# Conformer-conv statistics and output scaling in a hybrid decoder step: ScalarE's copies of blocks 5 and 7 moved, sums 56 columns wide, another order of the final scaling

## The chip, the cores and the metric

The kernel runs on one core of one Trainium2 chip. The metric is the time of one execution in microseconds on the device. The engines are TensorE (PE), VectorE (DVE), ScalarE (ACT), GpSimd (POOL) and SyncE (SP), which only issues DMAs here. Each engine works through its own instructions in order; they wait for one another by semaphores.

## The reference, cut to what matters

Four decoder layers, each a mixer and a squared-ReLU MLP, run over 256 prompt tokens and 8 sample tokens (T = 264 columns) with 1024 channels. The changed code is in the third layer's mixer, the Conformer conv, and in the norm at the very end.

```
def conformer_conv_mixer(xn, state, w_pw1, b_pw1, conv_w, conv_b, ln_g, ln_b, w_pw2, b_pw2):
    ag = jnp.einsum('bld,de->ble', xn, w_pw1) + b_pw1
    a, g = jnp.split(ag, 2, axis=-1)
    buf = jnp.concatenate([state, a * jax.nn.sigmoid(g)], axis=1)
    z = causal_dwconv(buf, conv_w) + conv_b          # 31 taps in each channel
    z = layer_norm(z, ln_g, ln_b)                    # mean and variance over the channels
    y = jnp.einsum('ble,ed->bld', jax.nn.silu(z), w_pw2) + b_pw2
    return y, buf[:, -(CONV_C_W - 1):]
...
return rms_norm(x, norm_final_g), ...
```

## The kernel before

Channels lie on the 128 partitions in eight blocks (0 to 7) and tokens along the columns. Every dense product is made of three TensorE products: weights and activations are each split into a high and a low part (`whi`, `wlo`, `xh`, `xl`). ScalarE makes the high part of a weight piece (L119), and VectorE or GpSimd the low part (L120). The program is written out by hand: in each engine's queue the instructions stand in the order in which the code issues them.

The stage of the change is the second half of `mixer_c`. Blocks 0 to 3 are convolved on VectorE, tap after tap (L855, `do_taps`). Blocks 4 to 7 are convolved on TensorE by 64 products (`conv_step`, L926, numbered n = 0 to 63), sixteen for each block, into two PSUM tiles `pairs[e, 0]` and `pairs[e, 1]`. The loop over n also hands out the other engines' work: it asks for so many taps at each n, for some leftover transposes and their copy to `rows` with two output DMAs on GpSimd's queue (L528, L829, L830), and for two pieces of weights (L119 and L120).

How a block leaves the TensorE convolution: in `leave(e)` ScalarE copies, from each of the two PSUM tiles, the half that lies on the wrong partitions to `over` (L954), and VectorE then adds both halves into `d` (L957). `apart(e)` subtracts a first estimate `mu` of the mean (L970 on VectorE, L972 on GpSimd; L975 for the eight sample columns), ScalarE squares the result (L977), and GpSimd adds up differences and squares over the blocks to `dsum` and `qsum` (L985). Blocks 3 and 7 are not added in; they go to the sums by themselves.

Then comes the norm. `token_sums` (L996) takes the sums over the channels on TensorE: the data are the weights of the product, and a block of ones, 28 or 56 columns wide, is streamed through. Few columns are needed; one of each width is read. VectorE turns the sums into mean and variance of each token (L1066 to L1072 and `rsqrt`, L255 to L259, whose root is ScalarE's). `to_channels` (L1003) spreads the mean (to `wide`) and the root (to `scale`) back over the partitions. `keep_clock` (L1183) issues products of ones with ones, 128 columns each, whose result nobody reads. ScalarE copies `wide` to `mu` (L1074); blocks 0 and 1 are corrected by VectorE from `wide` (L1081), the others by GpSimd from `mu` (L1083). `normed` and `gated` scale (L1088), take the sigmoid (L1090), multiply and split each block, and `wave` (L344 to L347) multiplies six output blocks by `w_pw2` as each input block arrives.

`root_table` is a one-element square root on ScalarE, which brings in the table of that function ahead of time; the sigmoid needs another table.

The end: after the last MLP the squares of the last block (`sq`) and of all others (`acc`) are summed in PSUM tile `ss` (L1284), the root `rt` is made, and six pieces of 128 x 512 are scaled (VectorE L1296 for the left halves from SBUF, ScalarE L1298 for the right halves from PSUM) and written out by SyncE's queue (L1300), the sample rows by ScalarE's (L1302).

Of the kernel before, what the change touches and what calls it, by code (L numbers as in the profile page):

```python
# [26 lines left out]
def decoder_trunk(ctx: ExitStack, tc: tile.TileContext, i, o):  # L27
# [796 lines left out]
    def mixer_c(ready):  # L824
# [122 lines left out]

        def leave(e):


            over = tmp.tile([P, SEQ], F32, tag="t1", name="over")
# [10 lines left out]
        total_ = {}  # L962

        def apart(e):
# [10 lines left out]
            nc.gpsimd.tensor_tensor(out=dt[e][:, SEQ:], in0=zs[:, e, :], in1=mu[:, SEQ:], op=ALU.subtract)  # L975
# [36 lines left out]
        for n, step in enumerate(steps):  # L1012
            conv_step(*step)
            if n == 15:
                leave(4)
                double(NB - 1)
# [6 lines left out]
            if n == 58:  # L1023
                root_table()
            for at, e in ((33, 5), (49, 6)):
# [28 lines left out]
        wide = psum()
        warm = ptp.tile([P, 512], F32, tag="tp", name="warm")
        keep_clock(5, warm)
        token_sums(sums[0], widths[0], 0, "d")
        token_sums(sums[1], widths[1], 0, "q")
        token_sums(sums[0], widths[0], 1, "d3")
        token_sums(sums[1], widths[1], 1, "q3")  # L1060
        token_sums(sums[0], widths[0], 2, "d7")
        token_sums(sums[1], widths[1], 2, "q7")
        dq = [
            ps[:, 0:9 * w].rearrange("p (b r w) -> p b r w", r=3, w=w)[:, :, :, 0] for ps, w in zip(sums, widths)
        ]
# [225 lines left out]
    for b in range(3):
        scale = rt[:, b:b + 1]
        for h, part in enumerate((ys[b][:, 0:512], back[1, b])):
            s = slice(h * 512, (h + 1) * 512)
            if h == 0:
                nc.vector.tensor_scalar_mul(ys[b][:, s], part, scale)  # L1296
            else:
                nc.scalar.activation(ys[b][:, s], part, AF.Copy, scale=scale)  # L1298
            if b < 2:
                nc.sync.dma_start(out=o["y_prompt"][0, b * P:(b + 1) * P, s], in_=ys[b][:, s])  # L1300
        if b == 2:
            nc.scalar.dma_start(out=o["y_sample"].rearrange("b l d -> (b l) d"), in_=ys[b][120:128, :])  # L1302


# [29 lines left out]
```

## Time and profile before

| | |
|---|---|
| median of 3 runs | 1105.05 us (1103.83 to 1105.38) |
| the profiled execution | 1103.74 us, its span 1102.0 us |
| mean granted TensorE clock | 0.992 |
| busy: PE, DVE, ACT, POOL | 99%, 67%, 56%, 18% |
| conv products on PE | 552.27 to 581.5 us |
| first product of `wave` | 598.04 us |
| last dense product | 1091.8 us |
| DMA during the sums | idle from 582 to 587 us |

The span runs from the first to the last instruction; the execution takes 1.7 us more. A stretch that PE spends on small products or waiting is what matters here, since elsewhere PE runs dense products without a gap. The columns of the table of stretches are busy time in us (and number of instructions) of each engine, then the granted clock, where 1.00 is 2.4 GHz and 0.50 is 1.2 GHz. In a timeline a row is a run of equal instructions: its start, the time that the run takes, engine, line, operation, tiles and count, and in brackets how long the engine was idle before it and what ended that.

### The profile page before, as it was taken

How to read it: one execution, taken by the hardware profiler on the slowest of the kernel's cores; microseconds unless marked ns; L12 is line 12 of the kernel's file. 1: busy time of each engine (PE TensorE's matmuls, PEld its weight loads, DVE VectorE, ACT ScalarE, POOL GpSimd, SP SyncE). 2: the span in 40 equal slices, each digit the busy share in tenths (PEclk: the TensorE clock that was granted, in tenths of full speed). 3: DMA queues.
4: the chain of work that ended last, by engine and by line, in shares of the span. 5: the costliest groups of instructions: out<-in, count | busy, mean ns of one | idle time of the engine just before them, and what ended most of it. 6: DMA issues, size and time to landing. Idle time of an engine off the chain costs nothing.

```text
span 1102.0 us, 21950 instructions
## 1 busy us (share of the span) xinstructions
PE 1090.5 (99%) x8801; PEld 1081.7 (98%) x8801; DVE 741.9 (67%) x1461; ACT 612.9 (56%) x1301; POOL 202.7 (18%) x372
## 2 busy tenths in 40 slices
PE   9999999999999999999999999999999999999997
PEld 8999999999999999999988999999999999999996
DVE  5788865566569657766986696566668678646731
ACT  6566653565458536555855585366545467535642
POOL 6213520100220001314993200000101120000010
PEclk9999999999999999999998999999999999999998
DMA  8766756555507666554531186555546565565511
GB/s 256 254 205 204 244 189 188 178 172 179 166 5 254 210 200 198 188 181 147 171 86 36 39 277 220 158 187 191 177 139 218 163 185 192 177 190 170 192 39 40
DMA packets 182639, 189.10 MB, mean 172 GB/s; under 512 B 3505, under 2 KB 180833, under 8 KB 182513
## 3 DMA queue, kind: packets, MB, share of 16 engines
q1 hardware_dynamic: 181865, 185.58, 53.2%
q0 software_dynamic: 656, 2.09, 0.6%
q8 instruction: 69, 1.13, 0.4%
q14 instruction: 33, 0.27, 0.1%
q10 hardware_dynamic: 16, 0.03, 0.0%
HBM read 186.27 MB, written 2.89 MB: 172 GB/s over the span
## 4 chain that ended last, share of the span: by engine, by line
PE 92%; DVE 3%; POOL 2%; ACT 1%; issue 0%; DVEq 0%; ACTq 0%; POOLq 0%
PE mm L160 28%; PE mm L162 28%; PE mm L161 28%; DVE mm L855 2%; POOL wlo L120 1%; PE mm L346 1%; PE mm L344 1%; PE mm L347 1%; PE mm L1183 1%; POOL mat L811 1%; PE warm L1183 0%; ACT mat L818 0%; PE mm L504 0%; PE st L276 0%; PE mm L698 0%
## 5 line engine op out<-in xcount | busy, mean ns | idle before, releaser
L119 ACT CAST whi<-wst 128x512 fp32r<-128x512 f32 x692 | 386.8, 616 | 249.7 <-PE mm L161 234.0
L120 DVE TENSOR_TENSOR wlo<-wst,whi 128x512 fp32r<-128x512 f32 x652 | 430.2, 704 | 103.2 <-ACT whi L119 95.3
L160 PE MATMUL mm<-xh,whi 128*128 128x264 f32 x1512 | 433.2, 286 | 0.0
L162 PE MATMUL mm<-xh,wlo 128*128 128x264 f32 x1512 | 429.2, 284 | 0.0
L161 PE MATMUL mm<-xl,whi 128*128 128x264 f32 x1512 | 428.0, 283 | 0.0
L160 PE MATMUL mm<-uh,whi 128*128 128x264 f32 x1168 | 332.5, 285 | 0.0
L162 PE MATMUL mm<-uh,wlo 128*128 128x264 f32 x1168 | 331.6, 284 | 0.0
L161 PE MATMUL mm<-ul,whi 128*128 128x264 f32 x1168 | 331.2, 284 | 0.0
L161 PEld LDWEIGHTS mm<-xl,whi 128*128 128x128 f32 x1512 | 285.0, 188 | 0.2
L160 PEld LDWEIGHTS mm<-xh,whi 128*128 128x128 f32 x1512 | 284.3, 188 | 0.4
L162 PEld LDWEIGHTS mm<-xh,wlo 128*128 128x128 f32 x1512 | 284.2, 188 | 0.0
L160 PEld LDWEIGHTS mm<-uh,whi 128*128 128x128 f32 x1168 | 220.0, 188 | 0.2 <-DVE xall L538 0.2
L161 PEld LDWEIGHTS mm<-ul,whi 128*128 128x128 f32 x1168 | 219.7, 188 | 0.0
L162 PEld LDWEIGHTS mm<-uh,wlo 128*128 128x128 f32 x1168 | 219.6, 188 | 0.0
L246 POOL TENSOR_TENSOR acc<-acc,sq 128x264 f32<-128x264 f32 x62 | 53.1, 856 | 551.2 <-ACT sq L245 550.4
L1129 DVE SCALAR_TENSOR_TENSOR t<-mm,r 128x264 f32<-128x264 f32 x128 | 54.8, 428 | 63.9 <-PE mm L162 63.7
L228 ACT CAST uh<-u 128x264 fp32r<-128x264 f32 x144 | 59.5, 413 | 33.0 <-DVE u L593 29.0
L1135 ACT ACTIVATE u<-t 128x264 f32<-128x264 f32 x128 | 54.0, 422 | 40.1 <-DVE t L1129 40.0
L230 DVE TENSOR_TENSOR ul<-u,uh 128x264 fp32r<-128x264 f32 x144 | 62.3, 433 | 0.3
L536 DVE TENSOR_TENSOR xall<-mm,xall 128x264 f32<-128x264 f32 x48 | 20.6, 429 | 58.7 <-PE mm L162 58.7
L233 ACT ACTIVATE xh<-xall,pv 128x264 fp32r<-128x264 f32 x56 | 28.9, 515 | 46.0 <-DVE xall L536 29.9
L120 POOL TENSOR_TENSOR wlo<-wst,whi 128x512 fp32r<-128x512 f32 x40 | 51.2, 1305 | 11.8 <-ACT whi L119 11.7
(236 smaller groups left out, 729.2 us busy)
## 6 DMA issues: line engine op xcount, KB each, us to landing
wst<-in_mlp_w_dram SPq DMA_DIRECT2D x128, 1024.0 KB, 5.6
wst<-in_a_w_in_dram SPq DMA_DIRECT2D x23, 1024.0 KB, 5.2
wst<-in_c_w_pw_dram SPq DMA_DIRECT2D x12, 1024.0 KB, 5.3
wst<-in_a_w_out_dram SPq DMA_DIRECT2D x8, 1024.0 KB, 5.2
xin<-in_x_prompt_dram SPq DMA_DIRECT2D x2, 512.0 KB, 6.8
wst<-in_b_w_group_dram SPq DMA_DIRECT2D x1, 1024.0 KB
out_y_prompt_dram<-ys SPq DMA_DIRECT2D x4, 256.0 KB, 2.3
stc<-in_state_conv_c_dram SPq DMA_DIRECT2D x2, 480.0 KB, 7.3
```

The source lines that it names most:

```text
L119: nc.scalar.copy(hi[:, k:k + 2], st[:, k:k + 2])
L120: (nc.gpsimd if u == 3 or (u, k) in ((0, 2), (0, 6)) else lo_engine[0]).tensor_tensor(out=lo[:, k:k + 2], in0=st[:, k:k + 2], in1=hi[:, k: ...
L160: nc.tensor.matmul(ps[:, :n], hi[:, k, s], xh[:, :n], start=first, stop=False)
L161: nc.tensor.matmul(ps[:, :n], hi[:, k, s], xl[:, :n], start=False, stop=False)
L162: nc.tensor.matmul(ps[:, :n], lo[:, k, s], xh[:, :n], start=False, stop=last)
L228: nc.scalar.copy(h, src)
L230: lambda: nc.vector.tensor_tensor(out=l, in0=src, in1=h.bitcast(F32), op=ALU.subtract)
L233: nc.scalar.activation(h, src, AF.Copy, scale=g)
L246: nc.gpsimd.tensor_tensor(out=acc, in0=acc, in1=sq, op=ALU.add)
L855: nc.vector.scalar_tensor_tensor(out=z(e), in0=gb[e][:, t:t + SEQ], scalar=col("ccw", t * 8 + e), in1=z(e), op0=ALU.mult, op1=ALU.add,)
L1129: nc.vector.scalar_tensor_tensor(out=t1, in0=ps[:, :T], scalar=0.0, in1=r, op0=ALU.max, op1=ALU.mult)
L1135: nc.scalar.activation(u, t1, AF.Square)
```

## The change

- In the conv loop ScalarE's copies to `over` are split from `leave` as `come_over(e)` and issued right when the block's last product is issued (n = 15, 31, 47, 63); VectorE's part of `leave` follows at n = 16, 36 and 49 and, for block 7, at the end as before. Before, both stood at n = 15, 33, 49 and at the end, there behind `apart(3)`.
- `apart(0)` and `apart(1)` move from n = 24 and 26 to 32 and 34, `apart(5)` from 38 to 37, `apart(6)` from 55 to 50. The sample columns of blocks 2, 3 and 7 are subtracted at n = 38. The square-root table is asked for at n = 49 instead of 58.
- All `token_sums` are 56 columns wide; there are 2 + 1 + 1 keep-clock products among them instead of 5 ahead, then 3 and 6 instead of 4 and 7. The PSUM tiles of the sums, of `wide` and of the keep-clock products change places.
- The sigmoid's table is asked for right behind the root, ahead of the copy of `wide`.
- At the end the two groups of sums get PSUM tiles of their own, four of the six scalings are VectorE's (one of them from PSUM), ScalarE issues one output DMA itself, and the sample rows go out by SyncE's queue.

```
         def come_over(e):
+            over_[e] = tmp.tile([P, SEQ], F32, tag="t1", name="over")
             for s in range(2):
                 own, other = (slice(h * HALF, (h + 1) * HALF) for h in (s, 1 - s))
-                nc.scalar.copy(over[own], pairs[e, s][other, 1:SEQ + 1])
+                nc.scalar.copy(over_[e][own], pairs[e, s][other, 1:SEQ + 1])
...
+            for at, e in ((15, 4), (31, 5), (47, 6), (63, 7)):
+                if n == at:
+                    come_over(e)
-            for at, e in ((33, 5), (49, 6)):
+            for at, e in ((36, 5), (49, 6)):
                 if n == at:
                     leave(e)
...
-            for at, e in ((22, 4), (24, 0), (26, 1), (38, 5), (55, 6)):
+            for at, e in ((22, 4), (32, 0), (34, 1), (37, 5), (50, 6)):
                 if n == at:
                     apart(e)
...
+        keep_clock(2, warm)
+        for at, e in enumerate(("", "3", "7")):
+            for ps, what in zip(sums, "dq"):
+                token_sums(ps, width, at, what + e)
+            if at < 2:
+                keep_clock(1, warm)
...
         rsqrt(v, root, rz)
+        nc.scalar.activation(scratch, ones[:, 0:1], AF.Sigmoid)
         nc.scalar.copy(mu, wide[:, :T])
-        keep_clock(4, warm)
+        keep_clock(3, warm)
         scale = pst.tile([P, T], F32, tag="st", name="scale")
         to_channels(scale, rz)
-        keep_clock(7, warm)
+        keep_clock(6)
...
-    ss = pst.tile([P, T], F32, tag="st", name="st")
+    ss = [pst.tile([P, T], F32, tag="st", name="st"), ptp.tile([P, 512], F32, tag="tp", name="st2")]
...
+    for b, h in ((0, 0), (0, 1), (1, 0), (1, 1), (2, 0), (2, 1)):
+        scalar = (b, h) in ((0, 1), (2, 1))
...
+            (nc.scalar if scalar else nc.sync).dma_start(
+                out=o["y_prompt"][0, b * P:(b + 1) * P, h * 512:(h + 1) * 512], in_=out
+            )
+    nc.sync.dma_start(out=o["y_sample"].rearrange("b l d -> (b l) d"), in_=ys[2][120:128, :])
```

ScalarE's queue in the conv loop, before, from the square of block 4 on (`gb4<-d4` is the square of block 4; `over` with two different PSUM tiles `mm` are the copies of one block, first block 5, then block 6):

```order
L977 ACTIVATE gb4_6681<-d4_7410 128x264
L977 ACTIVATE gb0_6677<-d0_7406 128x264
L977 ACTIVATE gb1_6678<-d1_7407 128x264
L528 COPY rows_7071<-tp_7519 128x512
L954 COPY over_7569<-mm_7503 64x256
L954 COPY over_7569<-mm_7529 64x256
L119 CAST whi_7392<-wst_7213 128x512
L977 ACTIVATE gb5_6682<-d5_7411 128x264
L119 CAST whi_7392<-wst_7213 128x512
L954 COPY over_7617<-mm_7564 64x256
L954 COPY over_7617<-mm_7593 64x256
```

The same queue at the same place after the change:

```order
L986 ACTIVATE gb4_6681<-d4_7410 128x264
L528 COPY rows_7071<-tp_7519 128x512
L955 COPY over_7551<-mm_7495 64x256
L955 COPY over_7551<-mm_7529 64x256
L986 ACTIVATE gb0_6677<-d0_7406 128x264
L986 ACTIVATE gb1_6678<-d1_7407 128x264
L119 CAST whi_7392<-wst_7213 128x512
L986 ACTIVATE gb5_6682<-d5_7411 128x264
L119 CAST whi_7392<-wst_7213 128x512
L955 COPY over_7614<-mm_7555 64x256
L955 COPY over_7614<-mm_7596 64x256
```

The copies of block 5 and the row copy have passed the squares of blocks 0 and 1; the copies of block 6 still stand behind the square of block 5 and a weight piece.

GpSimd's queue at the same place, before (L829 and L830 are the two output DMAs of `rows`):

```order
L972 TENSOR_TENSOR d0_7406<-d0_7406,mu_7405 128x256
L975 TENSOR_TENSOR d0_7406<-zs_6685,mu_7405 128x8
L985 TENSOR_TENSOR dsum_7536<-d4_7410,d0_7406 128x264
L985 TENSOR_TENSOR qsum_7538<-gb4_6681,gb0_6677 128x264
L972 TENSOR_TENSOR d1_7407<-d1_7407,mu_7405 128x256
L975 TENSOR_TENSOR d1_7407<-zs_6685,mu_7405 128x8
L985 TENSOR_TENSOR dsum_7536<-dsum_7536,d1_7407 128x264
L985 TENSOR_TENSOR qsum_7538<-qsum_7538,gb1_6678 128x264
L829 DMA out_new_conv_c_prompt_dram<-rows_7071 30x1024
L830 DMA out_new_conv_c_sample_dram<-rows_7071 8x1024
L120 TENSOR_TENSOR wlo_7393<-wst_7213,whi_7392 128x512
L972 TENSOR_TENSOR d5_7411<-d5_7411,mu_7405 128x256
```

And after:

```order
L829 DMA out_new_conv_c_prompt_dram<-rows_7071 30x1024
L830 DMA out_new_conv_c_sample_dram<-rows_7071 8x1024
L980 TENSOR_TENSOR d0_7406<-d0_7406,mu_7405 128x256
L970 TENSOR_TENSOR d0_7406<-zs_6685,mu_7405 128x8
L994 TENSOR_TENSOR dsum_7561<-d4_7410,d0_7406 128x264
L994 TENSOR_TENSOR qsum_7563<-gb4_6681,gb0_6677 128x264
L980 TENSOR_TENSOR d1_7407<-d1_7407,mu_7405 128x256
L970 TENSOR_TENSOR d1_7407<-zs_6685,mu_7405 128x8
L994 TENSOR_TENSOR dsum_7561<-dsum_7561,d1_7407 128x264
L994 TENSOR_TENSOR qsum_7563<-qsum_7563,gb1_6678 128x264
L120 TENSOR_TENSOR wlo_7393<-wst_7213,whi_7392 128x512
L980 TENSOR_TENSOR d5_7411<-d5_7411,mu_7405 128x256
```

The two DMAs have moved ahead of the work on blocks 0 and 1, which itself is issued eight products later.

TensorE's queue from the last conv product to the end of the sums, before (`sums` and `mm_7672` take the sums of the differences and of the squares):

```order
L1183 MATMUL warm_7675<-ones_85 128x128 x5
L996 MATMUL sums_7671<-ones_85,dsum_7536 128x28 x3
L996 MATMUL mm_7672<-ones_85,qsum_7538 128x56 x3
L996 MATMUL sums_7671<-ones_85,d3_7409 128x28 x3
L996 MATMUL mm_7672<-ones_85,gb3_6680 128x56 x3
L996 MATMUL sums_7671<-ones_85,d7_7413 128x28 x3
L996 MATMUL mm_7672<-ones_85,gb7_6684 128x56 x3
```

And after:

```order
L1196 MATMUL warm_7675<-ones_85 128x128 x2
L1005 MATMUL mm_7671<-ones_85,dsum_7561 128x56 x3
L1005 MATMUL mm_7672<-ones_85,qsum_7563 128x56 x3
L1196 MATMUL warm_7675<-ones_85 128x128
L1005 MATMUL mm_7671<-ones_85,d3_7409 128x56 x3
L1005 MATMUL mm_7672<-ones_85,gb3_6680 128x56 x3
L1196 MATMUL warm_7675<-ones_85 128x128
L1005 MATMUL mm_7671<-ones_85,d7_7413 128x56 x3
L1005 MATMUL mm_7672<-ones_85,gb7_6684 128x56 x3
```

Four keep-clock products stand ahead of and between the sums instead of five ahead, and the three groups of 28 columns have 56.

## Rows read from the trace of the kernel before

**Rows 1.** The page, its first part: busy time, share of the span and number of instructions of each engine.

```profile
PE 1090.5 (99%) x8801; PEld 1081.7 (98%) x8801; DVE 741.9 (67%) x1461; ACT 612.9 (56%) x1301; POOL 202.7 (18%) x372
```

**Rows 2.** Busy time of the engines in stretches around the sums: PE, PE's weight loads, DVE, ACT, POOL, then the granted clock.

```profile
584.00:586.00 2.00, 1.98 (x16) 1.88 (x16) 1.41 (x4) 1.50 (x3) 0.98 (x3) 1.00 0.00 0
...
587.00:588.00 1.00, 0.14 (x2) 0.03 (x1) 0.88 (x2) 0.00 (x0) 0.00 (x0) 0.52 0.08 16
...
597.00:598.00 1.00, 1.00 (x10) 1.00 (x9) 1.00 (x3) 0.42 (x2) 0.26 (x1) 0.86 0.00 0
```

**Rows 3.** The timeline of VectorE from block 5's way out to block 7's.

```profile
563.18 5.18 DVE L855 SCALAR_TENSOR_TENSOR mm<-gb,pv,mm 128x256 f32<-128x256 f32 x13
570.94 1.00 DVE L957 SCALAR_TENSOR_TENSOR d<-mm,pv,over 64x256 f32<-64x256 f32 x2 [2.58 <-ACT over L954]
...
578.36 1.00 DVE L957 SCALAR_TENSOR_TENSOR d<-mm,pv,over 64x256 f32<-64x256 f32 x2
...
582.66 0.42 DVE L970 TENSOR_TENSOR d<-mm,mu 128x256 f32<-128x256 f32 x1
...
585.09 0.42 DVE L970 TENSOR_TENSOR d<-mm,mu 128x256 f32<-128x256 f32 x1
586.46 1.00 DVE L957 SCALAR_TENSOR_TENSOR d<-mm,pv,over 64x256 f32<-64x256 f32 x2 [0.94 <-ACT over L954]
587.49 0.43 DVE L972 TENSOR_TENSOR d<-d,mu 128x256 f32<-128x256 f32 x1
```

**Rows 4.** The timeline of ScalarE in the same stretch.

```profile
569.94 0.57 ACT L528 COPY rows<-tp 128x512 f32<-128x512 f32 x1
570.53 0.76 ACT L954 COPY over<-mm 64x256 f32<-64x256 f32 x2
...
574.25 0.42 ACT L977 ACTIVATE gb<-d 128x264 f32<-128x264 f32 x1 [2.31 <-POOL d L975]
...
575.20 0.76 ACT L954 COPY over<-mm 64x256 f32<-64x256 f32 x2
...
583.62 1.28 ACT L266 ACT_TABLE_LOAD   x1
584.91 0.20 ACT L266 ACTIVATE scratch<-ones 128x1 f32<-128x1 f32 x1
...
586.05 0.76 ACT L954 COPY over<-mm 64x256 f32<-64x256 f32 x2
```

**Rows 5.** The timeline of GpSimd in the same stretch.

```profile
566.32 0.73 POOL L972 TENSOR_TENSOR d<-d,mu 128x256 f32<-128x256 f32 x1
...
571.04 0.56 POOL L829 DMA_DIRECT2D t_new_conv_c_prompt_dram<-rows  x1
571.59 0.50 POOL L830 DMA_DIRECT2D t_new_conv_c_sample_dram<-rows  x1
...
573.33 0.72 POOL L972 TENSOR_TENSOR d<-d,mu 128x256 f32<-128x256 f32 x1
...
583.23 0.74 POOL L985 TENSOR_TENSOR dsum<-dsum,d 128x264 f32<-128x264 f32 x1 [1.21 <-DVE d L970]
```

**Rows 6.** The timeline of TensorE from the conv's products 31 to 63 to the first product of `wave`. A product in full fp32 stands in it as two instructions, so x66 are 33 products and x6 three.

```profile
567.04 14.47 PE L926 MATMUL mm<-two,mat 128*128 128x257 f32 x66
581.34 1.28 PE L1183 MATMUL warm<-ones 128*128 128x128 f32 x10
584.02 0.85 PE L996 MATMUL sums<-ones,dsum 128*128 128x28 f32 x6 [1.40 <-POOL dsum L985]
584.72 0.88 PE L996 MATMUL mm<-ones,qsum 128*128 128x56 f32 x6
...
587.97 1.49 PE L996 MATMUL sums<-ones,d 128*128 128x28 f32 x6 [0.86 <-DVE d L972]
589.27 1.51 PE L996 MATMUL mm<-ones,gb 128*128 128x56 f32 x6
590.57 1.74 PE L1003 MATMUL mm<-ident,few 128*128 128x128 f32 x6
592.25 2.08 PE L1183 MATMUL warm<-ones 128*128 128x128 f32 x8
594.11 1.62 PE L1003 MATMUL scale<-ident,few 128*128 128x128 f32 x6
...
598.04 0.39 PE L346 MATMUL mm<-uh,whi 128*128 128x264 f32 x1
```

**Rows 7.** The timelines of ScalarE and VectorE between the sums and `wave`.

```profile
591.22 0.21 ACT L255 ACTIVATE few<-few 128x3 f32<-128x3 f32 x1 [2.79 <-DVE few L1072]
592.35 0.38 ACT L1074 COPY mu<-mm 128x264 f32<-128x264 f32 x1 [0.93 <-PE mm L1003]
...
592.83 0.77 DVE L1081 TENSOR_TENSOR d<-d,mm 128x264 f32<-128x264 f32 x2 [0.61 <-ACT mu L1074]
...
595.77 0.43 DVE L1088 TENSOR_TENSOR d<-d,scale 128x264 f32<-128x264 f32 x1 [2.17 <-PE scale L1003]
```

**Rows 8.** The timelines of VectorE and of SyncE's queue at the end: the second step of the last norm, and the four output DMAs of the prompt.

```profile
1093.87 0.16 DVE L1289 SCALAR_TENSOR_TENSOR rv<-st,rv 128x3 f32<-128x3 f32 x1
...
1095.82 1.83 SPq L1300 DMA_DIRECT2D out_y_prompt_dram<-ys  x4
```

**Rows 9.** The DMAs from 1094 to 1103 us: busy tenths of the 16 DMA engines in 40 equal slices (0.225 us each).

```profile
DMA  0000000000018999999999943464100000000000
```

More of the change, by code (lines that the diff above doesn't have):

```diff
@@ L946, in first_mean, with come_over, leave @@
             return means
-        def leave(e):
-            over = tmp.tile([P, SEQ], F32, tag="t1", name="over")
+        over_ = {}
+        def come_over(e):
+            over_[e] = tmp.tile([P, SEQ], F32, tag="t1", name="over")
             for s in range(2):
                 own, other = (slice(h * HALF, (h + 1) * HALF) for h in (s, 1 - s))
-                nc.scalar.copy(over[own], pairs[e, s][other, 1:SEQ + 1])
+                nc.scalar.copy(over_[e][own], pairs[e, s][other, 1:SEQ + 1])
+        def leave(e):
+            over = over_.pop(e)
             for s in range(2):
@@ L962, in mixer_c, with apart_samples @@
         total_ = {}
+        def apart_samples(e):
+            nc.gpsimd.tensor_tensor(out=dt[e][:, SEQ:], in0=zs[:, e, :], in1=mu[:, SEQ:], op=ALU.subtract)
         def apart(e):
@@ L974, in apart @@
                 )
-            nc.gpsimd.tensor_tensor(out=dt[e][:, SEQ:], in0=zs[:, e, :], in1=mu[:, SEQ:], op=ALU.subtract)
+            if not late:
+                apart_samples(e)
             sq = gb[e][:, :T]
@@ L1049, in mixer_c @@
         lag[0] = 0
-        widths = (28, 56)
-        sums = [pst.tile([P, T], F32, tag="st", name="sums"), psum()]
+        width = 56
+        sums = [psum(), psum()]
         few = tmp.tile([P, 4, 3], F32, tag="rs", name="few", bufs=1)
         md, v, root, rz = (few[:, k] for k in range(4))
[L1054 to L1065, printed above, removed]
+        wide = ptp.tile([P, 512], F32, tag="tp", name="wide")
+        warm = pst.tile([P, T], F32, tag="st", name="warm")
+        keep_clock(2, warm)
[4 more added lines that the diff above has]
+                keep_clock(1, warm)
+        dq = [ps[:, 0:9 * width].rearrange("p (b r w) -> p b r w", r=3, w=width)[:, :, :, 0] for ps in sums]
         nc.vector.tensor_reduce(out=md, in_=dq[0], op=ALU.add, axis=mybir.AxisListType.X)
@@ L1287, in decoder_trunk @@
     v, s = root_tiles(3)
-    mean(v, ss[:, 0:3])
-    nc.vector.scalar_tensor_tensor(out=v, in0=ss[:, 3:6], scalar=1.0 / D, in1=v, op0=ALU.mult, op1=ALU.add)
+    mean(v, ss[0][:, 0:3])
+    nc.vector.scalar_tensor_tensor(out=v, in0=ss[1][:, 0:3], scalar=1.0 / D, in1=v, op0=ALU.mult, op1=ALU.add)
     rsqrt(v, s, rt)
[L1291 to L1302, printed above, removed]
+    for b, h in ((0, 0), (0, 1), (1, 0), (1, 1), (2, 0), (2, 1)):
+        out, part, scale = ys[b][:, h * 512:(h + 1) * 512], back[1, b] if h else ys[b][:, 0:512], rt[:, b:b + 1]
+        scalar = (b, h) in ((0, 1), (2, 1))
+        if scalar:
+            nc.scalar.activation(out, part, AF.Copy, scale=scale)
+        else:
+            nc.vector.tensor_scalar_mul(out, part, scale)
+        if b < 2:
+            (nc.scalar if scalar else nc.sync).dma_start(
+                out=o["y_prompt"][0, b * P:(b + 1) * P, h * 512:(h + 1) * 512], in_=out
+            )
+    nc.sync.dma_start(out=o["y_sample"].rearrange("b l d -> (b l) d"), in_=ys[2][120:128, :])
 _INS = ['x_prompt', 'x_sample', 'state_conv_a', 'state_pool', 'state_conv_c', 'norm_mix_g', 'norm_mlp_g',
```

12 lines of the change are left out of this document (7 added, 5 removed).

## The prediction

> **What bounds the kernel now.** The page's first part came first: TensorE is busy 99% of the span [rows 1], so a change that leaves the dense products alone can gain only where TensorE waits, or where its small products are in the way. The timeline of TensorE shows such a place: the conv's product 63 ends at 581.5 us and the first product of `wave` starts at 598.04 [rows 6]. In these 16.5 us TensorE does only small sums and fillers, so the stage is a chain, and what ends last in it sets when the dense work goes on. From 598.04 to the last norm TensorE is full; I take it that a microsecond gained here stays.
>
> Three waits end last in the chain. VectorE's taps are its longest piece: VectorE stands still for 2.58 us ahead of block 5's way out and for 0.94 ahead of block 7's, both times for ScalarE's copies to `over` [rows 3]. TensorE waits 1.40 for `dsum` and 0.86 for block 7's differences [rows 6]. And the clock is granted in full at 584 to 586, after which it falls: 0.52 in the stretch 587 to 588, 0.86 in 597 to 598 [rows 2]. So 0.96 + 9 + 0.28 = 10.2 us run at 1.2 GHz, about from 587.0 to 597.3. The fall came after 3 us of sums of 28 and 56 columns, with the 1.40 us gap ahead of them; the rise came after some 7 us of 128-column products.
>
> **The way out of the blocks.** Before, the copies of block 5 started at 570.53 behind the squares of blocks 0 and 1 and the row copy [rows 4]. Now they stand behind the row copy alone. That copy can start when the transposes ahead of product 31 are done, some 567.2; it takes 0.57, so the copies start at 567.8, when product 31 (done at 567.5) [rows 6] is ready too. VectorE arrives after three further taps of 5.18 / 13 = 0.40 [rows 3], 568.36 + 1.2 = 569.6, and finds them done. The wait of 2.58 goes.
>
> A new wait comes next. On GpSimd the two output DMAs now stand ahead of block 0. They wait for the row copy until 567.85 and take 0.56 + 0.50 [rows 5], so block 0 starts at 568.95 and not at 566.32, 2.6 later. Queued behind are blocks 0, 1, a weight piece and block 5; since the DMAs no longer lie between 571.04 and 572.1, block 5 is 2.6 - 1.06 = 1.55 late (573.33 becomes 574.9). ScalarE squares it at 574.25 + 1.55 = 575.8, and the copies of block 6, still behind that square and a weight piece, start at 575.20 + 1.55 = 576.75 [rows 4]. VectorE would be there at 578.36 - 2.58 = 575.8 and gets the first half at 577.15: 1.35 of the 2.58 are given back. The cover for ScalarE's lateness was VectorE's own; it is gone. Bounds for this term: 0, if GpSimd keeps its old times, and the whole 2.58.
>
> So VectorE is 2.58 - 1.35 = 1.2 early from there: block 2's difference at 581.5 to 581.9, block 3's 583.9 to 584.3 [rows 3]. Block 7's copies now pass block 3's square and the table load; ready by 583.1 behind block 2's square, they no longer hold VectorE, so the 0.94 goes too and block 7's differences end at 587.92 - 1.2 - 0.94 = 585.8. The table load at n = 49 takes 1.28 + 0.20 [rows 4] while ScalarE would wait for block 6; the early sample columns fit into GpSimd's gaps. Both cost nothing.
>
> **The sums.** GpSimd's last `dsum` started at 583.23 and waited for block 2 [rows 5]; it now starts at 582.0, and TensorE, which used to begin at 584.02, begins at 582.75. The two fillers behind the conv end at 582.0 and are hidden. A group of three products took 0.70 with 28 columns and 0.85 to 0.88 with 56 [rows 6], so wider sums cost 0.15 a group for three groups if nothing else changes. Six groups of 0.85 and two fillers of 1.28 / 5 = 0.256 make 5.6. No input is late for its turn (block 7's turn comes at 586.6, its differences are there at 585.8), so TensorE itself bounds this piece, and the sums end at **588.35** where before they ended at 589.27 + 1.51 = 590.78. That holds at 2.4 GHz. At 1.2 GHz a group takes 1.30 of either width [rows 6] and a filler (594.11 - 592.25) / 4 = 0.465.
>
> Does the clock hold? The work is denser than before: no group of 28 columns is left, two 128-column fillers stand among the sums, the gap ahead of them is 0.75 rather than 1.40, and the 0.86 gap is gone. No row shows the clock under this mix; a denser one (conv and fillers) kept it, a thinner one lost it. I take that it holds, with odds of about two to one.
>
> **From the sums to `wave`.** Before, 598.04 - 590.78 = 7.26. After: the root starts 0.44 behind the sums and takes 0.21 [rows 7]. The sigmoid's table now comes next, 1.28 + 0.20 as for the other table [rows 4], and only then the copy of `wide`, 0.38. VectorE's correction of blocks 0 and 1 waits for that copy, as it did (592.83 behind 592.35 + 0.38) and takes 0.77 [rows 7]; the scaling starts 3.4 behind the sums. In TensorE's queue `wide` (1.68 at 1.2 GHz, taken as 0.84 at 2.4), three fillers (0.77) and `scale` (0.84) end after 2.45. So the table load, which used to lie hidden behind the copy, is now on the path, with 0.95 of it not covered by TensorE. From the scaling to the first product of `wave` stay 598.04 - 595.77 = 2.27. Sum 5.67; `wave` starts at 588.35 + 5.67 = **594.0**, 4.05 earlier. At 1.2 GHz the same queue needs 1.68 + 1.40 + 1.6 = 4.7, and behind it six fillers of 0.465 last longer than the 2.27: 7.0 to 7.5, nothing gained.
>
> On the table load a rule of the Trainium skill speaks against the move: "ScalarE: Activation LUTs", section "What ACT_TABLE_LOAD costs", gives about 1.28 us for the load and a further drain of about 1.38 for every switch. This trace agrees on the load, but shows the next instruction at 584.91, right behind it [rows 4], so I go by the trace.
>
> **The end.** With PSUM tiles of their own the first groups' mean no longer waits for the last block's squares, so the root is one VectorE step earlier, the step before the one at 1093.87: 0.16 and a start-up, about 0.2 [rows 8]. SyncE issued its four DMAs in 1.83, 0.46 each [rows 8]; one goes to ScalarE's queue now, so the last large one is issued some 0.5 earlier, though VectorE's fourth scaling (512 columns from PSUM, which no row shows: between the 0.42 of 256 columns from PSUM and twice that [rows 3]) eats part of it. The DMA engines are full from 1096.7 to 1099.2 and half busy to 1100.5 [rows 9], so transfers bound the rest. I take 0.5 gained; bounds -0.1 and 0.9.
>
> **Sum.** 1103.74 - 4.05 - 0.5 = 1099.2 against the profiled execution. That one lies 1.3 below the median of the three runs (1105.05). Where the clock falls may differ between executions, and in my forecast it doesn't fall; I put half of the 1.3 on top: **1099.8**.
>
> **Rivals.** (1) The clock falls all the same, within the sums or just behind. At the last four groups: 4 x 0.45 + 0.2 late, then 7.0 to 7.5, so `wave` starts at 597.3 to 597.8; just behind the sums, at 595.3. That gives 1100.5 to 1103.0, mostly near 1102. For it: TensorE still waits at 582.0, and sums of 56 columns were part of the mix that lost the clock. Chance 0.25.
>
> (2) The change doesn't do what it says: ScalarE's copies of block 6 come so late that VectorE gets back its whole 3.5 us. Block 7 ends at 587.9 as before, only the full clock remains: sums end at 589.7, `wave` 595.4, **1100.6**. For it: the chain from GpSimd through ScalarE to VectorE that I found above; against it: it takes 1.35 by the rows. Chance 0.08.
>
> (3) After the moved table load ScalarE stands still before it goes on, for as long as the load itself: 1.28 more on the path [rows 4], **1100.5**. Against it: the instruction at 584.91. Chance 0.05. The drain of the Trainium skill's "ScalarE: Activation LUTs", "What ACT_TABLE_LOAD costs", would be such a stall; by its figure the sum would be 1100.6, an estimate.
>
> (4) Slower: the clock falls late, in the gap ahead of `wave`. The fillers end at 588.35 + 2.45 + 6 x 0.256 = 592.3, `wave` starts at 594.0, so TensorE stands for 1.7 us, longer than the 1.40 before the fall in this trace. If 1.2 GHz then lasts for 10.2 us as here, dense products lose 5.1: 1099.2 + 5.1 = **1104.3**, slower than 1103.74; from 9.1 us at 1.2 GHz on, the whole gain is gone. More than 0.2% slower needs some 13.6 us. Against it: the six fillers come right before, and dense products follow. Chance 0.07.
>
> **Numbers.** Forecast 0.55. A measurement of this kernel can tell about 0.2%, 2.2 us, from no change: 1102.8 divides. Faster: 0.55 + 0.08 + 0.05 + 0.09 of rival 1 (a fall behind the sums) = 0.77; same: 0.16 of rival 1 and 0.02 of rival 4; slower 0.05. The range goes from 1099.2 - 1.35 - 0.4 = 1097.4 (no wait for block 6, end at its best) to 1103.4, rival 1 with some of the median's offset; rival 4 lies outside.
>
> **What would show it.** Right: no wait of VectorE ahead of block 5 and 7, one of about 1.4 ahead of block 6; GpSimd's DMAs near 568; sums ending near 588.3 at clock 1.00; the copy of `wide` behind a table load; `wave` at 594. Wrong: granted clock 0.50 anywhere between 582 and 605, a wait of TensorE among products 48 to 63 for a PSUM tile that block 6 still holds, or an end of the span more than 8.1 us behind the root (1102.0 - 1093.9).

## The result, and the profile after

| | before | after |
|---|---|---|
| median of 4 runs | 1104.94 us (1103.83 to 1105.38) | 1098.61 us (1098.28 to 1098.75) |
| ratio after to before | | 0.9945, 95% interval 0.9933 to 0.9957 |
| profiled execution | 1103.74 us, span 1102.0 | 1098.28 us, span 1096.5 |
| mean granted clock | 0.992 | 0.998 |
| product 31 to the first product of `wave` | 31.00 us | 26.32 us |

The changed kernel is 0.55% faster. TensorE's busy time fell by 5.2 us, from 1090.5 [rows 1] to 1085.3, with the same dense products. 4.85 of it lies between product 63 and `wave` (14.28 us busy there before, 9.43 after): its small products no longer run at half speed, and three fillers are fewer. The page, first part, after:

```profile
PE 1085.3 (99%) x8795; PEld 1076.7 (98%) x8795; DVE 743.2 (68%) x1462; ACT 612.9 (56%) x1301; POOL 202.8 (18%) x372
```

The three stretches of [rows 2] after (busy time of PE, PE's weight loads, DVE, ACT, POOL, then the granted clock). The clock is 1.00 in all of them, where 0.52 and 0.86 stood in the second and third:

```profile
584.00:586.00 2.00, 2.00 (x20) 2.00 (x20) 1.40 (x4) 0.85 (x2) 0.00 (x0) 1.00 0.03 8
...
587.00:588.00 1.00, 1.00 (x9) 0.88 (x8) 0.62 (x6) 0.24 (x2) 0.00 (x0) 1.00 0.00 0
...
597.00:598.00 1.00, 1.00 (x11) 1.00 (x9) 0.88 (x3) 1.00 (x4) 0.00 (x0) 1.00 0.00 0
```

All times of this trace stand 0.49 us earlier than their like of before when product 31 starts (566.55, where before had 567.04 [rows 6]); that came from earlier in the program, where the change touches nothing. Times are therefore compared from product 31 on. TensorE after, to hold against [rows 6]:

```profile
566.55 14.47 PE L926 MATMUL mm<-two,mat 128*128 128x257 f32 x66
...
582.61 0.88 PE L1005 MATMUL mm<-ones,dsum 128*128 128x56 f32 x6 [1.14 <-POOL dsum L994]
583.32 0.86 PE L1005 MATMUL mm<-ones,qsum 128*128 128x56 f32 x6
584.02 0.45 PE L1196 MATMUL warm<-ones 128*128 128x128 f32 x2
584.30 0.77 PE L1005 MATMUL mm<-ones,d 128*128 128x56 f32 x6
584.91 0.83 PE L1005 MATMUL mm<-ones,gb 128*128 128x56 f32 x6
...
585.86 0.77 PE L1005 MATMUL mm<-ones,d 128*128 128x56 f32 x6
586.47 0.83 PE L1005 MATMUL mm<-ones,gb 128*128 128x56 f32 x6
587.14 1.00 PE L1012 MATMUL wide<-ident,few 128*128 128x128 f32 x6
...
592.87 0.39 PE L346 MATMUL mm<-uh,whi 128*128 128x264 f32 x1 [1.22 <-ACT uh L228]
```

From one start to the next a group of sums (three products, x6) takes 0.61 to 0.71 us and a filler (one of the keep-clock products) 0.28. The groups of block 7 no longer wait. VectorE after, to hold against [rows 3] and [rows 7]:

```profile
568.96 0.99 DVE L962 SCALAR_TENSOR_TENSOR d<-mm,pv,over 64x256 f32<-64x256 f32 x2
...
576.95 1.00 DVE L962 SCALAR_TENSOR_TENSOR d<-mm,pv,over 64x256 f32<-64x256 f32 x2 [1.78 <-ACT over L955]
...
584.01 0.99 DVE L962 SCALAR_TENSOR_TENSOR d<-mm,pv,over 64x256 f32<-64x256 f32 x2
585.04 0.43 DVE L980 TENSOR_TENSOR d<-d,mu 128x256 f32<-128x256 f32 x1
...
589.84 0.77 DVE L1094 TENSOR_TENSOR d<-d,wide 128x264 f32<-128x264 f32 x2 [1.09 <-ACT mu L1087]
590.52 0.42 DVE L1101 TENSOR_TENSOR d<-d,scale 128x264 f32<-128x264 f32 x1
```

The waits of 2.58 and 0.94 are gone; one of 1.78 stands ahead of block 6, where there was none. What it waits for is in ScalarE's timeline, against [rows 4]: the copies of block 6 stand at 576.55 behind a weight piece and the square of block 5, which waited for GpSimd. Further down, the table load stands between root and copy:

```profile
575.59 0.42 ACT L986 ACTIVATE gb<-d 128x264 f32<-128x264 f32 x1 [2.68 <-POOL d L970]
...
576.55 0.76 ACT L955 COPY over<-mm 64x256 f32<-64x256 f32 x2
...
587.75 0.21 ACT L255 ACTIVATE few<-few 128x3 f32<-128x3 f32 x1 [1.82 <-DVE few L1084]
587.97 1.28 ACT L1086 ACT_TABLE_LOAD   x1
589.27 0.20 ACT L1086 ACTIVATE scratch<-ones 128x1 f32<-128x1 f32 x1
589.38 0.36 ACT L1087 COPY mu<-wide 128x264 f32<-128x264 f32 x1
```

And GpSimd's, against [rows 5]: its DMAs have come forward, block 5 has gone back.

```profile
567.63 0.56 POOL L829 DMA_DIRECT2D t_new_conv_c_prompt_dram<-rows  x1 [1.70 <-ACT rows L528]
...
574.65 0.74 POOL L980 TENSOR_TENSOR d<-d,mu 128x256 f32<-128x256 f32 x1
...
581.81 0.74 POOL L994 TENSOR_TENSOR dsum<-dsum,d 128x264 f32<-128x264 f32 x1 [0.65 <-DVE d L978]
```

The end, against [rows 8]: VectorE's last sum ahead of the norm, the second step of the norm, VectorE's one scaling from PSUM, and the issues of SyncE's queue.

```profile
1086.81 0.43 DVE L536 TENSOR_TENSOR xall<-mm,xall 128x264 f32<-128x264 f32 x1 [2.49 <-PE mm L162]
...
1088.68 0.16 DVE L1301 SCALAR_TENSOR_TENSOR rv<-st,rv 128x3 f32<-128x3 f32 x1 [0.81 <-PE st L1296]
...
1090.91 0.74 DVE L1310 TENSOR_SCALAR ys<-mm,rt 128x512 f32<-128x512 f32 x1
```

```profile
1090.63 1.74 SPq L1312 DMA_DIRECT2D out_y_prompt_dram<-ys  x3
1092.47 0.54 SPq L1315 DMA_DIRECT2D out_y_sample_dram<-ys  x1
```

That last sum stood here in the trace of before:

```profile
1091.81 0.43 DVE L536 TENSOR_TENSOR xall<-mm,xall 128x264 f32<-128x264 f32 x1 [2.49 <-PE mm L162]
```

From its start to VectorE's first scaling of `ys` it is 3.50 us before (to 1095.31) and 3.31 after (to 1090.12).

Part by part, profiled execution against profiled execution: 4.68 us between product 31 and `wave`, 0.49 ahead of product 31, and 0.32 from `wave` to the end of the span, together the 5.49 by which the span is shorter. The 0.32 are 0.5 gained at the end, less some 0.2 lost at the start of `wave` (below).

### The profile page after: what moved, and what is told of

Its sections match the earlier page's. It is cut to its first block, busy times and chain, and to the rows that moved or that the text cites. A ratio compares the mean times of both kernels' runs of the same rounds, so it can differ in the third digit from the quotient of the medians.

```text
span 1096.5 us, 21935 instructions
## 1 busy us (share of the span) xinstructions
PE 1085.3 (99%) x8795; PEld 1076.7 (98%) x8795; DVE 743.2 (68%) x1462; ACT 612.9 (56%) x1301; POOL 202.8 (18%) x372
## 4 chain that ended last, share of the span: by engine, by line
PE 97%; DVE 1%; POOL 1%; ACT 0%; issue 0%; DVEq 0%; POOLq 0%; ACTq 0%
PE mm L160 30%; PE mm L162 30%; PE mm L161 30%; PE mm L926 1%; PE mm L346 1%; PE mm L344 1%; PE mm L347 1%; PE mm L1196 1%; PE tp L524 0%; PE mm L1005 0%; PE mm L504 0%; DVE mm L855 0%; PE st L276 0%; PE mm L698 0%; PE mm L636 0%; PE mm L638 0%
## 5 line engine op out<-in xcount | busy, mean ns | idle before, releaser
L536 DVE TENSOR_TENSOR xall<-mm,xall 128x264 f32<-128x264 f32 x48 | 20.6, 430 | 59.3 <-PE mm L162 59.3
```

What stands on the lines that cost most here:

```text
L536: nc.vector.tensor_tensor(out=x[k], in0=ps[:, :T], in1=x[k], op=ALU.add)
```

## The experiments

Three questions were open. Which part holds the clock: the denser sums (fillers, width) or the shorter waits of the new order? Do the two waits that are left, the table load and the copies of block 6, cost what they seem to? Is the end worth 0.5 us?

Single executions of one kernel differ by up to 6 us (x2_sums, 1101.61 to 1107.71), partly for a reason that is not in this stage (last section). Where the medians can't tell, three lengths of the profiled execution are read instead: from the start of product 31 to `wave`, from there to VectorE's first scaling of `ys`, from there to the end of the span. They are those of one execution for each kernel. The ratios are to runs of the kernel before in the same measurement; its median was 1104.24 beside the x runs, 1104.64 beside the y runs and 1105.06 beside the z runs.

| kernel | median us | ratio to before, 95% | 31 to `wave` | `wave` to `ys` | `ys` to end |
|---|---|---|---|---|---|
| before | 1104.94 | 1 | 31.00 | 497.27 | 6.7 |
| after | 1098.61 | 0.9945 (0.9933 to 0.9957) | 26.32 | 497.25 | 6.4 |
| x1_order | 1101.47 | 0.9970 (0.9959 to 0.9981) | 28.45 | 497.21 | 6.7 |
| x2_sums | 1105.27 | 1.0005 (0.9994 to 1.0016) | 31.33 | 498.00 | 6.7 |
| x3_end | 1104.48 | 0.9998 (0.9990 to 1.0007) | 31.26 | 496.82 | 6.4 |
| x4_no_table | 1099.06 | 0.9949 (0.9937 to 0.9961) | 25.88 | 497.08 | 6.5 |
| y1_after | 1099.00 | 0.9952 (0.9940 to 0.9965) | 26.33 | 497.23 | 6.4 |
| y2_no_fill | 1103.11 | 0.9983 (0.9974 to 0.9993) | 30.84 | 496.92 | 6.5 |
| y3_narrow | 1101.27 | 0.9967 (0.9955 to 0.9980) | 26.30 | 497.12 | 6.5 |
| y4_over6 | 1097.92 | 0.9944 (0.9932 to 0.9957) | 25.50 | 497.25 | 6.4 |
| z1_over6_no_table | 1097.77 | 0.9937 (0.9926 to 0.9949) | 25.09 | 497.09 | 6.4 |
| z2_no_end | 1100.95 | 0.9971 (0.9956 to 0.9985) | 26.33 | 497.48 | 6.8 |
| z3_no_gap_fill | 1100.87 | 0.9963 (0.9951 to 0.9975) | 26.32 | 498.33 | 6.5 |
| z4_fill_wait | 1102.62 | 0.9981 (0.9968 to 0.9993) | 27.64 | 497.25 | 6.7 |

**x1_order: the loop's new order alone.** The old sums and the old end stay.

```
+            for at, e in ((15, 4), (31, 5), (47, 6), (63, 7)):
+                if n == at:
+                    come_over(e)
```

> The kernel before with the change's conv loop alone (copies to over, apart, sample columns, square-root table); sums, fillers, sigmoid table and end as before. First theory (the order shortens the way to the sums, the wider sums with fillers among them keep the clock): VectorE's waits of 2.58 and 0.94 us go, one of 1.4 to 1.8 comes, block 7's differences about 2 us earlier, but the clock still falls to 1.2 GHz for about 10 us, so 1.5 to 2.5 us faster than before, some 1102.5 to 1103.3. Second theory (TensorE's shorter waits keep the clock, whatever the sums' width): clock 1.00 through the sums and some 4.5 us faster, about 1100.3.

1101.47 us, between the two. The clock still falls, but later and for less: by the windows 0.52 + 6 + 0.32 = 6.8 us, where before had 10.2.

```profile
587.00:588.00 1.00, 1.00 (x9) 1.00 (x9) 0.50 (x4) 0.00 (x0) 0.00 (x0) 0.74 0.06 16
588.00:594.00 6.00, 6.00 (x26) 5.42 (x26) 2.45 (x11) 1.96 (x4) 3.45 (x5) 0.50 0.00 0
594.00:595.00 1.00, 1.00 (x9) 1.00 (x9) 0.95 (x1) 0.52 (x1) 0.80 (x2) 0.84 0.00 0
```

TensorE waits for `dsum` only 0.49 here, with five fillers ahead of the wait and none among the sums. The order alone does not hold the clock.

**x2_sums: the new sums and fillers alone,** in the old order, without the early table load.

```
+        width = 56
+        keep_clock(2, warm)
+            if at < 2:
+                keep_clock(1, warm)
```

> The kernel before with the change's sums, fillers and PSUM tiles alone; conv loop, sigmoid table and end as before, so VectorE's waits of 2.58 and 0.94 us stay and block 7's differences still come at about 587.9. First theory: the clock stays at 1.00, the sums end about 1.4 us earlier, wave starts some 3.5 us earlier, about 1101.4. Second theory: the waits ahead of the sums are as long as before, the clock falls all the same, within 0.7 us of before.

1105.27 us, no difference. The clock falls at 586.4, and for longer than before. That is the profiled execution; the twelve runs have mean clocks from 0.988 to 0.996, and two (1101.61 and 1102.56 us, at 0.996 and 0.995) lost less, so the fall is not the same in every execution. The row of the windows behind it:

```profile
587.00:600.00 13.00, 12.94 (x55) 11.85 (x54) 6.77 (x22) 5.29 (x11) 4.25 (x6) 0.50 0.00 0
```

The theory that the denser sums hold the clock by themselves falls with it. What they met is a wait of 2.14 us for `dsum`, longer than the 1.40 of before because three of the five fillers ahead of it are gone:

```profile
583.79 0.88 PE L996 MATMUL mm<-ones,dsum 128*128 128x56 f32 x6 [2.14 <-POOL dsum L985]
```

**x3_end: the end alone.**

```
-    ss = pst.tile([P, T], F32, tag="st", name="st")
+    ss = [pst.tile([P, T], F32, tag="st", name="st"), ptp.tile([P, 512], F32, tag="tp", name="st2")]
```

> The kernel before with the change's last norm, scaling and output DMAs alone. First theory: root 0.2 us earlier and the last landing 0.3 us earlier still, 0.5 us faster than before, about 1104.4. Rival: the transfers bound the end and the second queue disturbs the first, no difference within 0.2 us. The sums of the conv norm are as before, so the clock falls as before.

1104.48 us, no difference that the runs can tell. By the lengths the end is 0.3 us shorter behind the first scaling; the time from `wave` to it is 0.45 shorter than before, more than the root can give (0.2).

**x4_no_table: the changed kernel without the early table load.**

```
-        nc.scalar.activation(scratch, ones[:, 0:1], AF.Sigmoid)
         nc.scalar.copy(mu, wide[:, :T])
```

> The changed kernel without the sigmoid's early table load, which then stands behind the copy of wide as before the change. First theory (the load lies on the path from the root to the scaling): the copy of wide at about 588.1 instead of 589.4, the scaling then waits for scale on TensorE at about 590.1 instead of 590.52, wave 0.4 us earlier, about 1098.2. Rival: the load only moves to in front of the first sigmoid and costs there what it cost before, 1098.6 or slower.

`wave` comes 26.32 - 25.88 = 0.44 us earlier behind product 31: the early load costs, it doesn't pay. Left alone, the load starts behind the copy of `wide`, while ScalarE would wait for VectorE's scaling. The scaling then waits 0.71 for `scale` on TensorE, as the first theory has it. The medians (1099.06 here, 1098.61 and 1099.00 for the changed kernel) don't show 0.44.

**y1_after: the changed kernel once more,** unaltered.

> The changed kernel once more, unaltered, as the yardstick of its neighbours on the same chip. Both theories: 1098.3 to 1099.3 us, a granted clock of 1.00 from the convolution's last products through the sums to the wave, and the sums' first matmul some 16.1 us behind product 31.

1099.00 us, and 26.33 from product 31 to `wave`: the length repeats to 0.01.

**y2_no_fill: the changed kernel without the fillers at the sums.**

```
-        keep_clock(2, warm)
...
-            if at < 2:
-                keep_clock(1, warm)
```

> The changed kernel without the filler matmuls ahead of and between the sums (the two, the one and the one filler matmuls of keep_clock; the later ones stay). Theory 1 (the clock stays up because TensorE's pauses around the sums are filled, and the fillers are a part of that): the clock falls during or behind the sums as it does in the kernel with the order alone (6.8 us at half speed), about +3 us, 1101 to 1102.5 us. Theory 2 (the short wait and the wide sums hold it by themselves, and the fillers only take room): the clock stays at 1.00, the last groups wait for the squares of block 7 instead of for fillers, sums end about 0.3 us earlier, 1098.0 to 1098.8 us.

1103.11 us: theory 1. The wait for `dsum` is 0.43 longer (1.57 against 1.14), the clock falls at 586.8, inside the second group, and `wave` comes 4.5 us later. The four fillers, 1.1 us of TensorE's time at full clock, are worth some 4 us by the medians (1103.11 against 1099.00); the eleven runs reach from 1100.87 to 1105.69, and the profiled one is the slowest of them. The row of the windows behind the fall:

```profile
588.00:600.00 12.00, 11.94 (x52) 11.07 (x52) 4.96 (x17) 2.99 (x6) 4.29 (x6) 0.50 0.01 1
```

**y3_narrow: the changed kernel with the old widths.**

```
-        width = 56
+        widths = (28, 56)
```

> The changed kernel with the old widths (28 columns for the sums of the deviations, 56 for those of the squares), fillers and tiles as in the changed kernel. Theory 1 (the width itself keeps the clock up): with three of the six groups half as wide the clock falls around the sums, as with the order alone, +2 to +3 us, 1100.5 to 1102 us. Theory 2 (order and the place of the fillers hold it, width is only a cost): the clock stays at 1.00 and each of the three narrow groups is 0.1 to 0.25 us shorter, of which the wait for block 7 leaves about 0.2 us: 1098.0 to 1099.0 us.

Theory 2 as to the clock: it is 1.00 through the sums, and product 31 to `wave` takes 26.30. The sums need no width to hold it. As to the price it is wrong too: a group of 28 columns steps by 0.59 where one of 56 steps by 0.61, both right behind a filler, so nothing is won. In the profiled execution (1101.36) the loss does not come from this stage: product 31 starts at 569.81 against 566.81 in y1_after. 1.4 us of these 3.0 are there at 306 us already (the first product of L698 starts at 306.55 against 305.13); the rest comes with a fall of the clock at 310 us, told of below. Whether the old widths make that more likely can't be said from five runs.

**y4_over6: block 5's square behind block 6's copies on ScalarE.**

```
+            if n == 48:
+                squared(5)
```

> The changed kernel with the square of block 5 moved behind block 6's copies on ScalarE, so that these copies no longer stand behind a square that waits for GpSimd. Theory 1 (VectorE's 1.78 us wait for the copies of block 6 is what the path to the sums still pays; GpSimd's chain of sums is next at 0.65 us): the wait goes, GpSimd no longer waits 0.65 us for block 2, the sums' first matmul comes 0.6 us earlier, and so does the wave: 1098.0 us where the unaltered kernel has 1098.6, -0.6 us. Theory 2 (GpSimd's chain bounds the sums anyway, later squares of block 5 delay its sum): no change within 0.2 us. A rival to both: the shifted sums let the clock fall, +2 to +4 us.

`wave` comes 0.83 us earlier, a little more than the 0.6 expected, and the median is 1.1 lower in the same measurement, though the intervals of the two ratios overlap. TensorE's wait for `dsum` is 0.33, VectorE no longer waits ahead of block 6:

```profile
583.17 0.88 PE L1010 MATMUL mm<-ones,dsum 128*128 128x56 f32 x6 [0.33 <-POOL dsum L999]
```

```profile
576.58 1.00 DVE L962 SCALAR_TENSOR_TENSOR d<-mm,pv,over 64x256 f32<-64x256 f32 x2
```

**z1_over6_no_table: both cuts.**

```
+            if n == 48:
+                squared(5)
...
-        nc.scalar.activation(scratch, ones[:, 0:1], AF.Sigmoid)
```

> The changed kernel with block 5's square behind block 6's copies on ScalarE, and without the early table load behind the root: both cuts that the runs so far point to. Theory 1 (the table load on the way from root to the scale's copy costs 0.4 us, and the copies' wait 0.8 us, apart from each other): the wave's first product comes 1.2 us earlier behind product 31 than in the changed kernel, 25.1 us instead of 26.3, and the time is 1097.5 us. Theory 2 (they overlap: with the sums earlier, the table load no longer decides): 25.5 us as with the copies alone, 1098.0 us.

25.09 us from product 31 to `wave`: the two add up (0.83 + 0.44 = 1.27, measured 1.24). 1097.77 us, ratio 0.9937: this version has the lowest ratio to the kernel before of all, though its interval overlaps that of the changed kernel.

**z2_no_end: the changed kernel with the old end.**

> The changed kernel with the output's scaling and stores as they were before. Theory 1 (the end is worth about 0.35 us, as the two traces read from the last step of the norm to the span's end): 1099.3 us where the changed kernel has 1099.0, and 7.1 us from the last step of the norm to the end of the span, instead of 6.8. Theory 2 (the last landing of a store ends the span in either order): the same 6.8 us, and no difference.

Theory 1: from the last step of the norm to the end of the span it takes 7.15 us, y1_after 6.83, so 0.32 lie behind the norm. From VectorE's last sum (L536) to its first scaling it takes 3.51, y1_after 3.30: the root is 0.2 earlier. Together the end is worth about 0.5. Its runs reach from 1099.37 to 1105.04, so the median says nothing on 0.5. The two slowest, 1104.54 and 1105.04, have a mean clock of 0.990, the others 0.996 to 0.998.

**z3_no_gap_fill: no fillers ahead of `wave`.**

```
-        keep_clock(6)
```

> The changed kernel without the six filler matmuls between the scale's copy to the channels and the wave, so that TensorE is idle there for some 2.8 us instead of 1.2. Theory 1 (what it costs is pauses of TensorE that nothing fills, wherever they lie on this stretch): the clock falls at the wave's start, whose products then run at half speed, +2 to +4 us, 1101 to 1103 us. Theory 2 (only pauses around the sums do it, this late gap is too short): the clock stays at 1.00 and nothing changes, 1098.5 to 1099.3 us.

Theory 1: TensorE waits 2.75 us ahead of `wave`, the clock falls at 596.5, half a microsecond into it, and stays down for 0.5 + 2 + 0.9 = 3.4 us:

```profile
596.00:597.00 1.00, 0.97 (x6) 0.98 (x7) 1.00 (x2) 1.00 (x3) 1.00 (x3) 0.75 0.00 0
597.00:599.00 2.00, 2.00 (x11) 2.00 (x11) 1.86 (x5) 1.95 (x6) 0.75 (x1) 0.50 0.00 0
599.00:600.00 1.00, 1.00 (x7) 1.00 (x7) 0.72 (x3) 1.00 (x4) 0.00 (x0) 0.55 0.00 0
```

`wave` to `ys` takes 1.1 us more than in y1_after. So the fall that rival 4 feared does exist, at a fifth of the price that the rival gave it, and about half of the least expected here.

**z4_fill_wait: the old order, the new sums, and fillers enough for the old wait.**

```
-        keep_clock(2, warm)
+        keep_clock(9, warm)
```

> The kernel before with the changed sums (56 columns, fillers between them), and nine filler steps instead of two ahead of the sums, enough to fill the wait of 2.1 us for GpSimd that the old order leaves there. Theory 1 (the clock follows TensorE's pauses, and the new order holds it only because it shortens that pause): the clock stays at 1.00 through the sums, the wave comes some 4 us earlier behind product 31 than in the kernel with the sums alone, and the time is 1101 to 1102 us, though no copy has moved. Theory 2 (the clock follows something else of the order, or fillers of this kind don't count): it falls as with the sums alone, 1104.5 to 1106 us.

Theory 1. It is x2_sums with seven fillers more; no copy has moved. The wait for `dsum` shrinks to 0.55, the clock stays at 1.00 up to `wave`, and `wave` comes 3.7 us earlier than in x2_sums (27.64 against 31.33). The windows from the conv's end to `wave`:

```profile
583.00:586.00 3.00, 2.77 (x22) 2.50 (x20) 2.93 (x8) 0.59 (x3) 1.79 (x4) 1.00 0.41 144
586.00:590.00 4.00, 3.42 (x28) 3.23 (x28) 2.89 (x7) 2.56 (x5) 1.29 (x4) 1.00 0.02 4
590.00:594.00 4.00, 3.67 (x27) 3.31 (x28) 2.47 (x13) 1.91 (x4) 0.78 (x2) 1.00 0.00 0
594.00:597.00 3.00, 2.23 (x18) 1.87 (x16) 2.08 (x5) 1.51 (x4) 3.00 (x4) 1.00 0.00 0
```

Most of the gain in this stage can thus be had from fillers, with no copy moved: 31.00 - 27.64 = 3.4 of the 4.7 us (the sums are 56 columns wide here, but y3_narrow shows that the width is worth nothing). The rest, 1.3, is what the new order saves in waits, less the table load. The median, 1102.62, is only 2.4 below the 1105.06 of before in the same measurement; the nine runs reach from 1100.44 to 1107.07, with mean clocks from 0.990 to 0.997.

## Why the prediction was right, point by point

The sign and the mechanism held, the forecast of 1099.8 lies 1.2 above the median. 0.3 of that is the offset for the median (0.6 was put on top of the profiled execution, 0.33 was measured). 0.5 is the start of product 31, which the change does not touch: luck. The rest are the sizes below.

**The way out of the blocks.** Both waits went and the new one came, through the chain GpSimd, ScalarE, VectorE that the prediction named, but at 1.78 instead of 1.35: GpSimd's block 5 and with it the copies came 0.3 later than forecast and VectorE 0.14 earlier. Block 7's differences ended at 585.47, or 585.96 by the clock of before, for 585.8 forecast. VectorE got back 1.78 and not the whole 3.5, so rival 2 did not come about. y4_over6 shows that the wait is real and what it costs: 0.83 us.

**The sums.** This is the term that was mis-sized. They took 4.7 us (582.61 to 587.30) instead of 5.6, because a group of 56 columns was priced at its duration, 0.85 to 0.88, where from one start to the next it takes 0.61 to 0.71. The duration of such a group covers the end of its last product, which overlaps the next group; the 0.70 of 28 columns had been read as a step and the 0.88 as a duration. One step of 0.85 does stand in the trace of before, from the 56 columns at 584.72 [rows 6] to the group behind them:

```profile
585.57 0.85 PE L996 MATMUL sums<-ones,d 128*128 128x28 f32 x6
```

But that group needs block 3's differences, which VectorE ended at 585.09 + 0.42 = 585.51 [rows 3]: the 0.15 more were a wait, and no price of the width. y3_narrow shows that the width costs 0.02. TensorE started 0.35 later than forecast, so 0.56 of the 0.9 was left at the sums' end.

**Does the clock hold?** It did in both profiled executions of the changed kernel and, up to `wave`, in those of all versions that keep its loop and its fillers (x4_no_table, y3_narrow, y4_over6, the first three z runs). The odds of two to one were given for a reason that was only half right. The fillers ahead of and among the sums matter (y2_no_fill), and so does the length of the wait (x2_sums, z4_fill_wait); the missing groups of 28 columns do not (y3_narrow). x1_order, with five fillers ahead and none among the sums, fell behind a wait of only 0.49, which speaks for those among the sums; no run takes these out alone, nor moves the PSUM tiles alone. Neither the order nor the sums do it alone, so rival 1 was one part of the change away: x1_order, at 1101.47, lies in the range that this rival gave, 1100.5 to 1103.0. Nor is it shown that the clock always holds. Of the 31 runs with the changed kernel's loop, wide sums and fillers (after, x4_no_table, y1_after, y4_over6, z1_over6_no_table, z2_no_end), 29 have a mean clock of 0.995 or more, but two of z2_no_end have 0.990, the value of y2_no_fill's profiled execution. They were not profiled, so where the clock fell in them stays open.

**From the sums to `wave`.** 5.57 for 5.67. The table load is on the path as forecast, but for 0.44 by x4_no_table and not 0.95: `wide`, three fillers and `scale` had been put at 2.45 and took 2.8 (587.30 to 590.11), so they cover more of it. No stall follows it: the load ends at 589.25, the next instruction starts at 589.27. The drain that the Trainium skill gives in "ScalarE: Activation LUTs", "What ACT_TABLE_LOAD costs", is not seen in this trace either, and rival 3 falls.

**Rival 4** did not come about: the gap ahead of `wave` was 1.22 and not 1.7, and the fillers hold the clock across it (z3_no_gap_fill). Without them the fall costs 1.1 us rather than 5.1.

**The end.** 0.5 forecast, 0.5 by z2_no_end, 0.2 of it ahead of the first scaling, as forecast. The lengths from `wave` on are no better measure: x3_end gives 0.75 by them, but kernels with the same end scatter by 0.2 to 0.3.

**Not foreseen:** 0.49 us that product 31 came earlier, and 0.2 that `wave` lost at its start. The two pull opposite ways.

## What to carry to other kernels

Where a chain of small products stands between dense ones, look at the granted clock first: eleven fillers ahead of and among the sums instead of five ahead gave 3.4 us here (z4_fill_wait, profiled execution) and need no new order. In these runs they held the clock where 0.3 to 1.2 us of the wait was left, and did not where 2.14 was (x2_sums). Price a row of small products by the distance between starts, not by the duration of a group, and look at whether a wait sets that distance. And when a copy is moved forward on one engine, look for the next thing that still stands behind a wait in the same queue: the copies of block 6 did, and moving them as well brought `wave` another 0.8 us forward (y4_over6).

## What the hardware showed that was not expected

**The clock can fall without a pause of TensorE.** In seven of the fourteen profiled executions (x3_end, y2_no_fill, y3_narrow, all four of the last measurement) the clock fell near 309 us, in another layer's mixer, for 0.56 + 2 + 0.84 = 3.4 us. The profile shows no wait of TensorE there, nor in the microseconds ahead; the windows of y3_narrow:

```profile
308.00:310.00 2.00, 2.00 (x16) 1.89 (x16) 1.76 (x6) 1.26 (x4) 0.00 (x0) 1.00 0.04 8
310.00:311.00 1.00, 1.00 (x9) 1.00 (x9) 1.00 (x4) 0.59 (x2) 0.33 (x1) 0.72 0.00 0
311.00:313.00 2.00, 2.00 (x11) 2.00 (x11) 1.97 (x7) 0.00 (x0) 0.49 (x1) 0.50 0.00 0
313.00:314.00 1.00, 1.00 (x7) 1.00 (x7) 0.90 (x3) 0.25 (x1) 0.00 (x0) 0.58 0.00 0
```

What TensorE did ahead of it was small products here too: 22 of 24 to 128 columns (L698), 3.3 us long. In each of the seven the fall lies within 0.7 us of their end, before or after (in y3_narrow they end at 309.8 and the clock falls at 310.4). The other seven executions have the same products at the same place and no fall. Without it product 31 starts between 566.55 and 567.93, with it between 568.04 and 569.81; by y3_narrow it costs some 1.5 us, and stretches of the program ahead of it can cost 1.4 more. No kernel here changes that stretch, and the changed kernel's own two profiles don't have it; why it falls in one execution and not in another stays open. It is one source of the spread of the single runs.

**VectorE slows beside GpSimd.** At the start of `wave` GpSimd works through six subtractions, from 589.88 to 594.60, and three VectorE instructions in that time take 0.75, 1.01 and 0.98 us; the same ones take 0.43 once GpSimd is done. VectorE's timeline of the changed kernel there:

```profile
591.62 0.75 DVE L1115 TENSOR_TENSOR d<-gb,sgm 128x264 f32<-128x264 f32 x1
592.30 0.76 DVE L1101 TENSOR_TENSOR d<-d,scale 128x264 f32<-128x264 f32 x2
592.97 1.01 DVE L230 TENSOR_TENSOR ul<-d,uh 128x264 fp32r<-128x264 f32 x1
593.91 0.98 DVE L1115 TENSOR_TENSOR d<-gb,sgm 128x264 f32<-128x264 f32 x1
...
595.37 0.43 DVE L230 TENSOR_TENSOR ul<-d,uh 128x264 fp32r<-128x264 f32 x1
```

The two scalings at 592.30, which read one input from PSUM, take 0.38 each in the same stretch. The Trainium skill, "SBUF — State Buffer", section "SBUF: two separate sides", says that a VectorE instruction with two inputs in SBUF and a GpSimd instruction that reads SBUF take turns at a shared port; this trace agrees as to which ones slow down. x4_no_table agrees as well: GpSimd is done there at 593.78, and the instruction that takes 0.98 at 593.91 above takes 0.42 at 593.99. Before, GpSimd's subtractions were over some 0.8 us ahead of `wave`; now that the chain is shorter they run 1.7 us into it. The slow instruction ends at 594.89, ScalarE's cast of the second block follows at 594.92, and the second block of `wave` starts at 595.39, 2.52 us behind the first where it was 2.34 before.
